# A decoder trunk on one core: early splits of two weights in buffers of their own, and a first chunk loaded in halves

## The chip, the core and the metric

The kernel runs on one core of one Trainium2 chip. The metric is the device time of one execution in microseconds (us), as the median of several executions. TensorE (PE) multiplies matrices, and PEld is its loading of weights; ScalarE (ACT), VectorE (DVE) and GpSimd (POOL) compute on tiles; SyncE (SP) issues most transfers. Each engine works through its instructions in the order in which the program lists them, and waits on semaphores for what other engines or transfers owe it.

## The reference, cut to what matters

Two layers of a decoder with 512 tokens of 1024 features: layer 0 mixes tokens with latent attention, layer 1 with a gated recurrence; each goes on through a SwiGLU block and a gated extra embedding. The change lies at the start of layer 0's attention:

```python
down = x @ w_dqkv                                   # 512x1024 @ 1024x576
c_q  = rms_norm(down[..., :256], q_norm)
c_kv = rms_norm(down[..., 256:512], kv_norm)
k_rope = apply_rope(down[..., 512:], cos, sin)      # 64 columns
q = (c_q @ w_uq).reshape(B, S, H, 128 + 64)         # the 64: rotary queries
kv = (c_kv @ w_ukv).reshape(B, S, H, 128 + 128)     # the second 128: values
...
s = (q_nope . k_nope + q_rope . k_rope) * scale     # causal softmax, then @ v, then @ w_o
```

## The kernel before

Every fp32 product is done as three TensorE products of split operands: `split` (L178) makes a rounded copy `hi` on ACT (L179) and the rest `lo = src - hi` on DVE (L180), and `mm3` (L203 to L205) adds hi·hi, lo·hi and hi·lo. A group of weights is one `unit` (L188): a 128x1024 tile `raw` (3 buffers) is loaded by SP (L191) and split into `whi` and `wlo`. These have 5 buffers each, which the chunks of the down projection and all later units take in turn. So a unit's `lo` frees its `raw` buffer for the load three units on, and a unit's `hi` needs the products of the unit five back to be done.

`mla` starts with the down projection. The contraction over 1024 features is cut into 8 chunks (kc) of 128; for each, SP loads `xT` (128x512, L580) and `w_dqkv` (128x576, L582), ACT and DVE split both, and PE adds 8 groups of three 288-column products (4 token tiles t by 2 column halves n) into 8 banks of PSUM (`dq`: tp, tp, sc, sc, ps, ps, ps, wg). The last three chunks (NL = 3) run token tile by token tile (L594 to L596), so that the sums of t = 0 are ready first. In the same loop each tile is normed: ACT squares and sums both halves (L605), DVE and POOL make the inverse root (`rstd`: L211 and L213), DVE scales each half into `cn` (L610) and copies the rotary key (L612, tile `kr`). Two tiles later, `to_feat` (L307) transposes `cn` on PE, and `csink` splits the result into `cT` (ACT L179 and DVE L180, names `big<-tp`).

After that loop the source has the units of rotary queries (`wr`, from `mla_w_qr`) and of values (`wv`, two from `mla_w_v`), then for each t the rotary queries (`rope_q`: 6 products, rotated at L554 to L560) and the values (12 products), and then, head by head, units of `mla_w_qk` (here qk0, qk1, ...), scores and softmax. The rotary tables (L259 to L285) use a sine on ACT, for which a table is loaded (ACT_TABLE_LOAD, 1.28 us).

The code doesn't say when each engine does its share: a scheduler reorders each engine's instructions when the program is built, from dependences, buffers and its own estimates. The order on each engine is fixed from then on. Buffers of the tag "mb" (`mid`) are a second set; before the change the attention uses the first of them for the rotary tables, and the others only for the softmax (`turn`).

## Time and profile before

| what | us |
|---|---|
| median of 3 executions (lowest, highest) | 1292.88 (1292.80, 1293.83) |
| the profiled execution, own time | 1295.24 |
| its span, first to last instruction | 1293.5 |
| PE busy in it (share of the span) | 1269.2 (98%) |
| DVE, ACT, POOL busy | 802.1 (62%), 665.7 (51%), 128.0 (10%) |
| PE waits before its first product | 5.6 |
| PE waits between 11 and 42 us (norms of the down projection) | 0.48 and 1.29 |

The profiled execution took 2.36 us more than the median; differences are worked out within it and then applied to the median. PE is the engine that sets the time, so the question at each step is when PE stands still and what releases it.

### The profile page before, as it was taken

Reading aid. Unit: us, or ns where it says so; the run is one execution under the profiler, and the core shown is the slowest. Engines: PE = TensorE matmul, PEld = TensorE weight load, DVE = VectorE, ACT = ScalarE, POOL = GpSimd, SP = SyncE. Lnnn points to the kernel's source line nnn. Section 1 sums busy time; section 2 is a strip of 40 time slices with the busy share of each in tenths; the row PEclk is TensorE's granted clock in tenths of the full one; section 3 lists DMA queues with packets and bytes.
Section 4 is the critical chain, followed back from the end, with each engine's and each line's share of the span. In section 5 each row is a group of like instructions: output and inputs, shape, how many; then the busy total and the mean of one; then the engine's idle time right before and its main releaser. Section 6 shows DMA issues by size and latency. Waiting matters only on the chain.

```text
span 1293.5 us, 20112 instructions
## 1 busy us (share of the span) xinstructions
PE 1269.2 (98%) x7900; PEld 1138.4 (88%) x7900; DVE 802.1 (62%) x1454; ACT 665.7 (51%) x1150; POOL 128.0 (10%) x165
## 2 busy tenths in 40 slices
PE   8999999999999999999999999999999999999998
PEld 8778879999999888888888888888899999888887
DVE  7998477777765333853367778358676676433463
ACT  6666367776775222533334344337677766322352
POOL 0200021111110000100001110002111111000000
PEclk9999999999999999999999999999999999999999
DMA  7124157878775223232321222337888886323231
GB/s 229 66 66 138 47 142 172 203 185 184 175 186 153 92 94 111 93 111 69 116 96 51 64 82 66 97 83 157 215 185 187 185 185 160 126 94 96 92 98 49
DMA packets 49055, 161.70 MB, mean 125 GB/s; under 512 B 5824, under 2 KB 6080, under 8 KB 48704
## 3 DMA queue, kind: packets, MB, share of 16 engines
q1 hardware_dynamic: 36000, 123.71, 29.9%
q0 software_dynamic: 12960, 36.71, 16.4%
q8 instruction: 62, 1.02, 0.3%
q14 instruction: 33, 0.27, 0.1%
HBM read 158.30 MB, written 2.10 MB: 124 GB/s over the span
## 4 chain that ended last, share of the span: by engine, by line
PE 86%; DVE 5%; DMA 4%; ACT 2%; issue 2%; POOL 1%; SPq 0%; POOLq 0%; DVEq 0%; ACTq 0%
PE ps L203 19%; PE ps L204 19%; PE ps L205 19%; PE sc L203 3%; PE sc L204 3%; PE sc L205 3%; PE wg L204 3%; PE wg L203 3%; PE wg L205 2%; DMA raw<-ffn_w_in 2%; PE sc L859 2%; PE tp L307 2%; PE ps L433 2%; DMA wlo<-ffn_w_in 2%; PE tp L204 2%
## 5 line engine op out<-in xcount | busy, mean ns | idle before, releaser
L180 DVE TENSOR_TENSOR wlo<-raw,whi 128x1024 fp32r<-128x1024 f32 (+1 forms) x125 | 149.2, 1195 | 206.7 <-ACT whi L179 204.3
L179 ACT ACTIVATE whi<-raw 128x1024 fp32r<-128x1024 f32 (+1 forms) x125 | 129.4, 1036 | 242.2 <-PE wg L205 125.6
L203 PE MATMUL ps<-big,whi 128*128 128x256 f32 (+1 forms) x640 | 202.3, 316 | 1.7 <-ACT part L444 1.7
L205 PE MATMUL ps<-big,wlo 128*128 128x256 f32 (+1 forms) x640 | 198.7, 311 | 0.0
L204 PE MATMUL ps<-big,whi 128*128 128x256 f32 (+1 forms) x640 | 198.7, 310 | 0.0
L203 PE MATMUL ps<-whi,big 128*128 128x512 f32 (+2 forms) x440 | 171.1, 389 | 0.5 <-ACT t L605 0.5
L205 PE MATMUL ps<-whi,big 128*128 128x512 f32 (+2 forms) x440 | 168.2, 382 | 0.0
L204 PE MATMUL ps<-wlo,big 128*128 128x512 f32 (+2 forms) x440 | 167.9, 382 | 0.0
L203 PEld LDWEIGHTS ps<-big,whi 128*128 128x128 f32 x640 | 122.4, 191 | 6.7 <-ACT part L444 1.9
L205 PEld LDWEIGHTS ps<-big,wlo 128*128 128x128 f32 x640 | 122.2, 191 | 6.5
L204 PEld LDWEIGHTS ps<-big,whi 128*128 128x128 f32 x640 | 122.4, 191 | 4.8
L205 PEld LDWEIGHTS ps<-whi,big 128*128 128x128 f32 x440 | 83.0, 189 | 16.0
L203 PEld LDWEIGHTS ps<-whi,big 128*128 128x128 f32 x440 | 83.1, 189 | 14.9 <-ACT t L605 0.7
L204 PEld LDWEIGHTS ps<-wlo,big 128*128 128x128 f32 x440 | 83.1, 189 | 14.4
L180 DVE TENSOR_TENSOR wlo<-ma,whi 128x1024 fp32r<-128x1024 f32 x40 | 49.0, 1224 | 35.4 <-ACT whi L179 35.4
L213 POOL TENSOR_TENSOR rr<-rv,mhalf 128x1 f32<-128x1 f32 (+2 forms) x28 | 27.9, 997 | 419.5 <-DVE rv L211 419.5
L205 PE MATMUL ps<-whi,ma 128*128 128x512 f32 x164 | 64.2, 392 | 0.0
L204 PE MATMUL ps<-wlo,ma 128*128 128x512 f32 x164 | 64.2, 391 | 0.0
L203 PE MATMUL ps<-whi,ma 128*128 128x512 f32 x164 | 64.0, 390 | 0.0
L186 POOL DMA_DIRECT2D ma<-ffn_w_in x40 | 34.3, 857 | 246.6 <-DVE big L465 158.0
L444 ACT ACTIVATE part<-ps 128x256 f32<-128x256 f32 x120 | 44.4, 374 | 25.8 <-PE ps L205 25.2
L184 ACT ACTIVATE whi<-raw 128x1024 fp32r<-128x1024 f32 x50 | 52.8, 1061 | 7.7 <-DMA raw<-ffn_w_in 4.3
(325 smaller groups left out, 3154.2 us busy)
## 6 DMA issues: line engine op xcount, KB each, us to landing
raw<-ffn_w_in SPq DMA_DIRECT2D x88, 512.0 KB, 5.0
wlo<-ffn_w_in POOLq DMA_DIRECT2D x48, 512.0 KB, 7.3
raw<-ffn_w_down SPq DMA_DIRECT2D x44, 512.0 KB, 3.5
ma<-ffn_w_in POOLq DMA_DIRECT2D x40, 256.0 KB, 6.9
raw<-ple_w_gate SPq DMA_DIRECT2D x16, 512.0 KB, 3.6
raw<-hgrn_w_fq SPq DMA_DIRECT2D x16, 512.0 KB, 3.6
raw<-mla_w_o SPq DMA_DIRECT2D x8, 512.0 KB, 3.6
raw<-hgrn_w_v SPq DMA_DIRECT2D x8, 512.0 KB, 4.4
```

Of the source, the lines that this page charges most:

```text
L179: self.nc.scalar.activation(hi, src, AF.Copy)
L180: self.nc.vector.tensor_tensor(out=lo, in0=src, in1=hi.bitcast(F32), op=ALU.subtract)
L184: self.nc.scalar.activation(hi, raw, AF.Copy)
L186: self.nc.gpsimd.dma_start(lo, src, accum_op=ALU.add)
L203: mm(ps, a[0], b[0], start=start, stop=False, skip_group_check=more)
L204: mm(ps, a[0], b[1], start=False, stop=False, skip_group_check=more)
L205: self.last = mm(ps, a[1], b[0], start=False, stop=stop, skip_group_check=more).ins
L213: nc.gpsimd.tensor_tensor(out=r, in0=v, in1=self.mhalf[:, :n], op=ALU.pow)
L307: self.nc.tensor.transpose(out=ps[:, c * P:(c + 1) * P], in_=src[:, c * P:(c + 1) * P], identity=self.ident)
L433: nc.tensor.matmul(ps[q][:, :N], w[q][k][:, kc * P:(kc + 1) * P], xT(f"A{half + 1}{kc // 4 + 1}")[m][:, kc % 4], start=kc + k + m == 0, st ...
L444: copy = lambda dst, src: nc.scalar.activation(dst, src[:, :N], AF.Copy)
L859: nc.tensor.matmul(ps[:, c * P:(c + 1) * P], X[:, c * P:(c + 1) * P], pair_view(cs[0][:, :, 1, :], cs[1][:, :, 0, :]), start=True, stop=True)
```

## The change

Two things are edited. First, chunk kc = 0 is loaded in four transfers rather than two, in the order: tokens 0 to 255 of `xT`, columns 0 to 287 of `w_dqkv`, columns 288 to 575, tokens 256 to 511. Each half is split by itself, and PE's 24 products follow in groups of two token tiles and one column half. Second, `unit` takes a tag: the unit of rotary queries and the first unit of values are split into buffers of the tag "mb" instead of `whi` and `wlo`, and both are written ahead of the norm loop; the second unit of values stays where it was.

```diff
@@ -185,12 +185,15 @@
         self.nc.scalar.activation(lo, hi.bitcast(F32), AF.Copy, scale=-1.0)
         self.nc.gpsimd.dma_start(lo, src, accum_op=ALU.add)
 
-    def unit(self, src, adding=False):
+    def unit(self, src, adding=False, tag=None):
 
         raw = self.wp.tile([P, 1024], F32, tag="raw", bufs=3, name=self.nm("raw"))
         self.nc.sync.dma_start(raw, src)
-        hi = self.wp.tile([P, 1024], F32R, tag="whi", bufs=5, name=self.nm("whi"))
-        lo = self.wp.tile([P, 1024], F32R, tag="wlo", bufs=5, name=self.nm("wlo"))
+        if tag:
+            hi, lo = self.mid([P, 1024], F32R, tag), self.mid([P, 1024], F32R, tag)
+        else:
+            hi = self.wp.tile([P, 1024], F32R, tag="whi", bufs=5, name=self.nm("whi"))
+            lo = self.wp.tile([P, 1024], F32R, tag="wlo", bufs=5, name=self.nm("wlo"))
         if adding:
             self.split_dma(hi, lo, raw, src)
         else:
@@ -577,13 +580,27 @@
         ws = []
         for kc in range(KC):
             xk = xr[kc // 4][:, kc % 4]
+            raw = self.wp.tile([P, 576], F32, tag="raw", bufs=3, name=self.nm("raw"))
+            w = [self.wp.tile([P, 576], F32R, tag=g, bufs=5, name=self.nm(g)) for g in ("whi", "wlo")]
+            ws.append(w)
+            if kc == 0:
+
+                tok, col = (slice(0, 256), slice(256, 512)), (slice(0, 288), slice(288, 576))
+                for z, src, cs in ((xk, i["xT"][:, 0], tok[0]), (raw, i["mla_w_dqkv"][0], col[0]),
+                                   (raw, i["mla_w_dqkv"][0], col[1]), (xk, i["xT"][:, 0], tok[1])):
+                    nc.sync.dma_start(z[:, cs], src[:, cs])
+                    if z is xk:
+                        self.split(*xT(0, cs), xk[:, cs])
+                    else:
+                        self.split(w[0][:, cs], w[1][:, cs], raw[:, cs])
+                for ts, n in (((0, 1), 0), ((0, 1), 1), ((2, 3), 0), ((2, 3), 1)):
+                    for t in ts:
+                        self.mm3(dq[t][n][:, :288], xT(0, slice(t * P, (t + 1) * P)), [z[:, col[n]] for z in w], True, False)
+                continue
             nc.sync.dma_start(xk, i["xT"][:, kc])
-            raw = self.wp.tile([P, 576], F32, tag="raw", bufs=3, name=self.nm("raw"))
             nc.sync.dma_start(raw, i["mla_w_dqkv"][kc])
             self.split(*xT(kc), xk)
-            w = [self.wp.tile([P, 576], F32R, tag=g, bufs=5, name=self.nm(g)) for g in ("whi", "wlo")]
             self.split(w[0], w[1], raw)
-            ws.append(w)
             if kc < KC - NL:
                 for t in range(NT):
                     down(kc, t, w)
@@ -594,6 +611,8 @@
         cT = [self.slot([P, 4, S], F32R) for _ in range(2)]
         csink = lambda t, n, ps: self.split(*(z[:, :, t * P:(t + 1) * P] for z in cT), ps)
         cns = []
+        wr = self.unit(i["mla_w_qr"], tag="mb")
+        wv = [self.unit(i["mla_w_v"][0], tag="mb")]
         for t in range(NT):
             for kc in range(KC - NL, KC):
                 down(kc, t, ws[kc])
@@ -617,8 +636,7 @@
 
         qs = [self.slot([P, 4, S], F32R) for _ in range(2)]
         vt = (Rows(self, F32R), Rows(self, F32R))
-        wr = self.unit(i["mla_w_qr"])
-        wv = [self.unit(i["mla_w_v"][n]) for n in range(2)]
+        wv.append(self.unit(i["mla_w_v"][1]))
 
         def rope_q(t):
             ps = self.bank()
```

The helpers move down by 3 lines: L178 to L213 stay in the split and become L206 to L208 (`mm3`), L214 and L216 (`rstd`), L310 (`to_feat`), L624 (squares), L629 (scaling), L631 (copy), L288 (sine).

What the scheduler makes of it differs from the kernel before only in the first 440 or so of PE's 7,000 rows, and on ACT and DVE in the rows up to the attention; POOL's order is the same, and SP's has one more load at the start. Three places:

ACT, from the last split of the down projection to the first split of `cT`. In the kernel before (`whi_513` are the rotary-query weights, `whi_519` and `whi_525` the two units of values, `tp_105` and `tp_106` the sums of t = 0, `sc` of t = 1, `ps_109` and `ps_110` of t = 2):

```order
L179 ACTIVATE whi_513<-raw_511 128x1024
L179 ACTIVATE whi_519<-raw_517 128x1024
L285 ACT_TABLE_LOAD
L285 ACTIVATE mb_218<-ma_219 128x128
L605 ACTIVATE t_54_386,ss_385<-tp_105 128x256
L605 ACTIVATE t_54_386,ss_385<-tp_106 128x256
L285 ACTIVATE mb_218<-ma_219 128x128
L605 ACTIVATE t_59_417,ss_416<-sc_107 128x256
L605 ACTIVATE t_59_417,ss_416<-sc_108 128x256
L605 ACTIVATE t_65_455,ss_454<-ps_109 128x256
L605 ACTIVATE t_65_455,ss_454<-ps_110 128x256
L179 ACTIVATE big_365<-tp_447 128x4x128
```

and after the change (`mb_375`: rotary queries, `mb_381`: first values, `whi_531`: second values, `whi_750`: qk0):

```order
L624 ACTIVATE t_60_404,ss_403<-tp_105 128x256
L288 ACT_TABLE_LOAD
L288 ACTIVATE mb_224<-ma_225 128x128
L179 ACTIVATE mb_375<-raw_373 128x1024
L624 ACTIVATE t_60_404,ss_403<-tp_106 128x256
L288 ACTIVATE mb_224<-ma_225 128x128
L179 ACTIVATE mb_381<-raw_379 128x1024
L624 ACTIVATE t_65_435,ss_434<-sc_107 128x256
L179 ACTIVATE whi_531<-raw_529 128x1024
L624 ACTIVATE t_65_435,ss_434<-sc_108 128x256
L179 ACTIVATE big_371<-tp_465 128x4x128
L179 ACTIVATE whi_750<-raw_748 128x1024
```

The squares of t = 0 stood behind both early splits and the table load, one after another; now the first of them comes first, the splits stand between the squares, and the split of qk0, a load that comes later, ends this piece and stands right ahead of the squares of t = 2 (`ps_109`, `ps_110`), which are the next two rows.

DVE, around the scaling of t = 2 (`ps_109`, `ps_110`), before:

```order
L211 TENSOR_SCALAR rv_458<-ss_454 128x2
L610 SCALAR_TENSOR_TENSOR t_68_462<-ps_109,rr_460,ma_98 128x256
L180 TENSOR_TENSOR big_366<-tp_447,big_365 128x4x128
L612 COPY ma_364<-ps_109 128x32
L610 SCALAR_TENSOR_TENSOR t_68_462<-ps_110,rr_460,ma_98 128x256
L612 COPY ma_364<-ps_110 128x32
L180 TENSOR_TENSOR wlo_526<-raw_523,whi_525 128x1024
L180 TENSOR_TENSOR wlo_745<-raw_742,whi_744 128x1024
L180 TENSOR_TENSOR big_366<-tp_485,big_365 128x4x128
L211 TENSOR_SCALAR rv_496<-ss_492 128x2
```

and after (`wlo_751` is qk0's `lo`):

```order
L180 TENSOR_TENSOR big_372<-tp_465,big_371 128x4x128
L214 TENSOR_SCALAR rv_476<-ss_472 128x2
L180 TENSOR_TENSOR wlo_751<-raw_748,whi_750 128x1024
L629 SCALAR_TENSOR_TENSOR t_74_480<-ps_109,rr_478,ma_98 128x256
L631 COPY ma_370<-ps_109 128x32
L629 SCALAR_TENSOR_TENSOR t_74_480<-ps_110,rr_478,ma_98 128x256
L631 COPY ma_370<-ps_110 128x32
L180 TENSOR_TENSOR big_372<-tp_503,big_371 128x4x128
```

The second values' and qk0's `lo` came behind the scaling of t = 2; now they come ahead of it: qk0's is between the statistics (`rv_476`) and the scaling, and the second values' was moved further up, ahead of the scaling of t = 1.

PE, around the transposes of t = 2, before (`ps_531` are rotary queries of tile 0, `ps_547` and `ps_556` its values, `tp_565` and `tp_606` the transposes of t = 2 and 3):

```order
L203 MATMUL ps_547<-whi_519,big_365 128x512
L204 MATMUL ps_547<-wlo_520,big_365 128x512
L205 MATMUL ps_547<-whi_519,big_366 128x512
L203 MATMUL ps_547<-whi_519,big_365 128x512
L204 MATMUL ps_547<-wlo_520,big_365 128x512
L205 MATMUL ps_547<-whi_519,big_366 128x512
L307 MATMUL tp_565<-ident,t_68_462 128x128 x4
L307 MATMUL tp_606<-ident,t_74_500 128x128 x2
L203 MATMUL ps_556<-whi_525,big_365 128x512
L204 MATMUL ps_556<-wlo_526,big_365 128x512
```

and after (`tp_503`: t = 1, `tp_571`: t = 2, `ps_537` and `ps_553`: rotary queries and first values of tile 0):

```order
L206 MATMUL wg_112<-whi_362,big_103 128x288
L207 MATMUL wg_112<-wlo_363,big_103 128x288
L208 MATMUL wg_112<-whi_362,big_104 128x288
L310 MATMUL tp_503<-ident,t_68_442 128x128 x4
L310 MATMUL tp_571<-ident,t_74_480 128x128 x2
L206 MATMUL ps_537<-mb_375,big_371 128x512
L207 MATMUL ps_537<-mb_376,big_371 128x512
L208 MATMUL ps_537<-mb_375,big_372 128x512
L206 MATMUL ps_537<-mb_375,big_371 128x512
L207 MATMUL ps_537<-mb_376,big_371 128x512
L208 MATMUL ps_537<-mb_375,big_372 128x512
L206 MATMUL ps_553<-mb_381,big_371 128x512
```

Before, the transposes of t = 2 came behind the twelve products of rotary queries and first values; now their first two stand ahead of these, right behind the four of t = 1. The transposes of t = 0 (`tp_465`) moved the other way, by nine products, and stand in two pairs with two products between them.

## Rows read from the trace of the kernel before

**Rows 1.** The page's chain of work that ended last, followed back from the end: shares of the span by engine.

```profile
PE 86%; DVE 5%; DMA 4%; ACT 2%; issue 2%; POOL 1%; SPq 0%; POOLq 0%; DVEq 0%; ACTq 0%
```

**Rows 2.** The view of waits of PE over the whole span (rows of four; columns: what waited, for whom, us in all, times, longest).

```profile
PE ps L433 <- DMA wlo<-ffn_w_in: 6.0, 4, 2.9
...
PE tp L307 <- DVE ma L612: 1.3, 1, 1.3
```

**Rows 3.** The timeline of the first 11 us (columns: start, duration, engine, line, operation, out<-in, shape, and in brackets the idle time before and what ended it; L179 is the `hi` split, L180 the `lo`).

```profile
0.74 0.39 SPq L580 DMA_DIRECT2D big<-xT  x1
...
1.18 0.42 SPq L582 DMA_DIRECT2D raw<-mla_w_dqkv  x1
...
4.19 0.63 ACT L179 ACTIVATE big<-big 128x512 fp32r<-128x512 f32 x1 [1.96 <-DMA big<-xT]
...
4.88 0.68 ACT L179 ACTIVATE whi<-raw 128x576 fp32r<-128x576 f32 x1
...
5.62 0.85 PE L203 MATMUL tp<-whi,big 128*128 128x288 f32 x2 [5.62 <-ACT whi L179]
...
7.87 0.76 DVE L180 TENSOR_TENSOR wlo<-raw,whi 128x576 fp32r<-128x576 f32 x1 [0.92 <-ACT whi L179]
...
9.69 0.44 PE L204 MATMUL ps<-wlo,big 128*128 128x288 f32 x1
...
9.93 0.34 PE L205 MATMUL ps<-whi,big 128*128 128x288 f32 x1
...
10.78 0.29 PE L205 MATMUL wg<-whi,big 128*128 128x288 f32 x1
...
10.92 0.30 PE L203 MATMUL tp<-whi,big 128*128 128x288 f32 x1
```

**Rows 4.** The timeline from 22 to 34 us, the norms of t = 0 and t = 1 (same columns; `t<-tp` at L605 is a square of t = 0, L610 a scaling, L307 a group of four transposes).

```profile
24.21 1.23 DVE L180 TENSOR_TENSOR wlo<-raw,whi 128x1024 fp32r<-128x1024 f32 x1 [0.38 <-ACT whi L179]
...
24.86 1.06 ACT L179 ACTIVATE whi<-raw 128x1024 fp32r<-128x1024 f32 x1 [0.69 <-DMA raw<-mla_w_v]
...
25.46 2.45 SPq L191 DMA_DIRECT2D raw<-mla_w_qk  x2
25.58 0.29 PE L205 MATMUL tp<-whi,big 128*128 128x288 f32 x1
...
25.95 1.28 ACT L285 ACT_TABLE_LOAD   x1
...
27.24 0.31 ACT L285 ACTIVATE mb<-ma 128x128 f32<-128x128 f32 x1
...
27.46 0.37 ACT L605 ACTIVATE t<-tp 128x256 bf16<-128x256 f32 x1
...
27.95 0.38 ACT L605 ACTIVATE t<-tp 128x256 bf16<-128x256 f32 x1
...
28.58 0.16 DVE L211 TENSOR_SCALAR rv<-ss 128x2 f32<-128x2 f32 x1
...
28.82 0.71 POOL L213 TENSOR_TENSOR rr<-rv,mhalf 128x2 f32<-128x2 f32 x1 [27.02 <-DVE rv L211]
...
29.57 0.48 DVE L610 SCALAR_TENSOR_TENSOR t<-tp,rr,ma 128x256 f32<-128x256 f32 x1 [0.83 <-POOL rr L213]
...
30.92 0.60 PE L307 MATMUL tp<-ident,t 128*128 128x128 f32 x4
...
33.74 0.60 PE L307 MATMUL tp<-ident,t 128*128 128x128 f32 x4
```

**Rows 5.** The timeline from 34 to 40 us, with the two stops of PE after the down projection (same columns; `ps<-whi,big` of 512 columns are products of rotary queries and values, L612 copies the rotary key out of a PSUM bank).

```profile
34.49 0.18 DVE L612 COPY ma<-ps 128x32 f32<-128x32 f32 x1
...
34.82 0.47 PE L203 MATMUL ps<-whi,big 128*128 128x512 f32 x1 [0.48 <-ACT t L605]
...
35.07 2.36 DVE L180 TENSOR_TENSOR wlo<-raw,whi 128x1024 fp32r<-128x1024 f32 x2
...
37.66 0.60 PE L307 MATMUL tp<-ident,t 128*128 128x128 f32 x4
...
38.18 0.70 POOL L213 TENSOR_TENSOR rr<-rv,mhalf 128x2 f32<-128x2 f32 x1 [4.73 <-DVE rv L211]
...
38.91 0.48 DVE L610 SCALAR_TENSOR_TENSOR t<-ps,rr,ma 128x256 f32<-128x256 f32 x1 [0.49 <-POOL rr L213]
...
39.55 0.41 PE L307 MATMUL tp<-ident,t 128*128 128x128 f32 x2 [1.29 <-DVE ma L612]
```

**Rows 6.** The view of transfers in the first 60 us (columns: tile<-tensor, queue, operation, times, size of one, median us from issue to landing).

```profile
raw<-mla_w_qk SPq DMA_DIRECT2D x4, 512.0 KB, 4.2
...
raw<-mla_w_o SPq DMA_DIRECT2D x1, 512.0 KB, 3.6
```

**Rows 7.** Busy time in stretches of the span (columns: stretch, its length, busy us and instructions of PE, PEld, DVE, ACT and POOL, the clock granted to PE as a share of 2.4 GHz, share of time and rate of the transfers).

```profile
70.00:130.00 60.00, 59.28 (x368) 49.26 (x367) 51.47 (x169) 39.49 (x116) 1.04 (x1) 1.00 0.29 95
194.00:198.00 4.00, 4.00 (x24) 4.00 (x23) 1.14 (x2) 1.93 (x3) 0.00 (x0) 0.57 0.08 14
890.00:892.00 2.00, 2.00 (x20) 2.00 (x19) 0.00 (x0) 0.63 (x2) 0.00 (x0) 1.00 0.97 195
```

**Rows 8.** The timeline of PE at two long stops in the SwiGLU blocks (columns as in rows 3).

```profile
193.63 1.50 PE L433 MATMUL ps<-big,wlo 128*128 128x256 f32 x8 [2.88 <-DMA wlo<-ffn_w_in]
...
888.57 1.21 PE L433 MATMUL ps<-big,wlo 128*128 128x256 f32 x8 [2.47 <-DMA wlo<-ffn_w_in]
```

## The prediction

> **What bounds the kernel now.** I read the chain of work that ended last first: 86% of it is TensorE (PE) [rows 1]. PE's order is fixed when the program is built, so a change is worth what it takes from, or adds to, the times at which PE stands still. The view of waits says where those are: 5.6 us ahead of the first product, 6.0 us for weights in the SwiGLU blocks, and in the part that the change touches one of 1.3 us [rows 2]; the timeline adds one of 0.48 us [rows 5]. From the first product to 34 us there is none, which is the cover under which all norms of the first two token tiles run today. 1293.5 us of span contain some 1269 us of PE work, and the change alters none of that.
>
> **The start.** PE's first product needs `xT` and the `hi` of the first weights. The loads are issued at 0.74 and 1.18; `xT`'s `hi` starts at 4.19 and the weights' at 4.88, 0.69 later, takes 0.68, and PE starts at 5.62 [rows 3]. With halves the first product needs only 288 columns. Their `hi` is about half of 0.68, or 0.37 if I take a 256-column ACT row (a square [rows 4]), so 0.31 is saved whatever the transfers do. The transfers: 544 KB lie ahead of the first product before, 272 KB after; half of the 0.69 between the two landings is 0.35 if they share the rate evenly, none if the landing is set by latency alone, and the whole 0.69 at most. So PE starts 0.3 to 1.0 us earlier; I take 0.7 (0.31 + 0.35, rounded). The Trainium skill (DMA: Bandwidth & Descriptors, section "Measured (HBM→SBUF, 128 partitions, SWDGE, issued from GpSimd)") speaks against this edit: it asks to batch transfers to 1 MiB or more, since smaller ones lose rate. If that ruled here, the halves would land no sooner than the wholes, 0.3 would be left of the 0.7, and the sum below would be +2.0. The rows speak for overlap instead: two loads issued 0.44 apart land 0.69 apart, both over 3 us after their issue.
>
> A second doubt is the clock. PE's products start 0.24 us apart at 9.69 and 9.93, and 0.14 apart at 10.78 and 10.92 [rows 3]: the granted clock goes from 1.2 to 2.4 GHz at about 10 us. If that moment moves with PE's start, all of the 0.7 is kept; if it stands still, the extra work is done at 1.2 GHz and half is kept. Bounds of the term: **-0.2 to -1.0, taken -0.7**. Two more SP issues at some 0.45 us push all later loads of the projection back by 0.9. The cover: chunk 1 is split by 7.87 + 0.76 = 8.63 and first used at 10.92 [rows 3], 2.3 us of slack, of which 1.6 (0.9 and the earlier start) is used up, so nothing is lost. Without cover it would cost those 0.9.
>
> **The two stops of today go: -1.77.** The 0.48 us stop is before the first 512-column product at 34.82, whose PSUM bank is freed by the key copy of t = 2 at 34.49 + 0.18 [rows 5]. The 1.29 us stop is before the transposes of t = 3 at 39.55; behind it stands a chain of 2.36 us of `lo` splits on DVE from 35.07, ahead of the statistics, POOL's 0.70 and the scaling at 38.91 [rows 5]. In the new order neither place exists as it was. What is late next is worked out now, from the same rows, with PE 0.7 earlier.
>
> **The new chain of the norms.** t = 0's last product is 25.58 + 0.29 - 0.7 = 25.2 [rows 4]. ACT then does: square (0.49 from 27.46 to 27.95) to 25.7, table load 1.28 to 27.0, sine (0.22 to its next) 27.2, `hi` of rotary queries 1.06 to 28.25, second square 28.75, second sine 29.0, `hi` of first values 30.0. Before the change both `hi` were over when the squares began; now 1.06 of split stands between the two squares of t = 0, whose sum feeds one statistic. DVE: `lo` of rotary queries 1.23 to 29.5; statistic 29.7; POOL 0.71 to 30.5; first scaling to 31.0; then `lo` of first values, 1.23, to 32.2, which the new order puts between the two scalings; second scaling to 32.7.
>
> PE comes to the transposes of t = 0 at 30.92 - 0.7 + 9 products of 0.135 = 31.4: the first pair is ready. The second pair, two products and 0.3 of transposes later, is due at 32.0 and ready at 32.7: **0.7 new wait**. For t = 1, seven products on, PE is due at 32.7 + 0.3 + 0.9 = 33.9. DVE's statistic is at 32.9, but the `lo` of the second values (1.23) stands ahead of the scalings: 34.2, first pair 34.7, second 35.2: 0.8 and 0.2 of wait, of which I take **0.8** in all, since one DVE instruction begins up to 0.1 before the other ends.
>
> t = 2 is the dear one. Its transposes now come right behind those of t = 1, where PE is at 35.3; before, twelve products stood between (34.82 to 37.66, 2.84 us [rows 5]). Its squares wait on ACT behind qk0's `hi`. qk0's load needs the `raw` buffer that the `lo` of rotary queries frees: in the trace the load is issued at 25.46, as that `lo` ends (24.21 + 1.23) [rows 4]. Now that `lo` ends at 29.5, so the load lands 3.6 to 4.2 us later [rows 6], at 33.1 to 33.7. ACT is then free of `cT`'s first split at about 33.6; `hi` to 34.7, two squares to 35.7. DVE has `cT`'s `lo` in between, statistic at 36.1, then qk0's `lo`, 1.23, to 37.3 (POOL's 0.70 runs beside it), scaling to 37.8. PE has been idle since 35.3: 2.5 by this sum, **taken 2.3** with the same overlaps. On ACT's queue behind the waiting `hi` are those squares, qk1's `hi` and `cT`; nothing else of PE's hangs on them in that time.
>
> t = 3: PE goes on with the twelve products, is due at 37.6 + 0.3 + 2.84 + 0.3 = 41.0; on ACT, qk1's and qk2's `hi`, one each ahead of a square, and on DVE qk1's `lo` make the scaling ready at 41.3 to 42.0: 0.3 to 1.0, **taken 0.6**. Together **+4.4** (3.4 to 5.2), against 1.77 before.
>
> **Later.** `whi` and `wlo` are free of two units, so the splits of `mla_w_qk` run ahead. From 70 to 130 us PE stands still for 60.00 - 59.28 = 0.72 [rows 7]. Some of it is such splits: -0.3 taken, -0.7 at best; +0.5 (the size of a stop like that of [rows 5]) if the new order makes one more.
>
> **The sum:** -0.7 - 1.77 + 4.4 - 0.3 = +1.63. The profiled execution of 1295.24 becomes 1296.9; the median of 1292.88 becomes **1294.5**.
>
> **Rivals.** (a) The chain keeps up: the squares and scalings are early enough and only the gains stay: -0.7 - 1.77 = -2.5, 1290.4. For it: today's chain shows slack, as t = 0's scaling at 29.57 is 1.3 ahead of PE at 30.92 [rows 4]. Against: three instructions of over 1 us that stood before or behind this chain now stand in it. (b) Old stops turn into new ones of the same size, and only the start is gained: 1292.2; this needs t = 2's stop to be 0.3 or less in place of 2.3, so the load of qk0 early or its `hi` short. (c) The slower end: t = 2's stop lowers PE's clock. After a stop of 2.88 us the granted clock was 0.57 over 4 us [rows 7, 8], so 4 x 0.43 = 1.7 us were lost; after one of 2.47 us it stayed at 1.00 [rows 7, 8]. At 2.3 it stays; this rival decides from somewhere between these two, and with the waits of 0.7 and 0.8 shortly before it could do so sooner: +1.63 + 1.7 = +3.3, 1296.2. (d) The loads of qk0 and qk1 land later than the 3.9 that I took in the middle of 3.6 and 4.2 (these are medians of four loads and of one, 0.6 apart [rows 6]): at 0.5 more for each, both stops behind them grow, +1.0, 1295.5.
>
> **How the numbers follow.** Forecast 0.50, (a) 0.12, (b) 0.12, (c) 0.13, (d) 0.13. A measurement of this kernel can tell 0.2%, 2.6 us, from no change: below 1290.3 is faster, above 1295.5 slower. Faster: half of (a), 0.06. Slower: (c), half of (d), and 0.03 of the forecast's upper end: 0.23. Same: 0.71. The forecast by itself has bounds from -0.3 (smallest waits, best start) to +3.0, with 1293.3 to 1295.8 as its likely part; the range of 8 in 10 leaves out (a) and the far end of (c) and (d): 1291.9 to 1296.6.
>
> **What would show it.** PE's first product at 4.6 to 5.3 and the clock's step. Then PE waits on L310 (transposes), released by DVE, four of them or more between 30 and 42 us with 4.4 in sum, the longest of 2 to 2.5 us just ahead of the rotary queries; qk0's load issued near 29.5; its `hi` waiting for it, and t = 2's squares behind. No wait of that size there, or the squares ahead of 34 us, would make the forecast wrong; a granted clock near 0.5 after 38 us would show (c), a longer wait of ACT for `raw` (d).

## The result, and the profile after

| what | before | after |
|---|---|---|
| median of 9 executions (lowest, highest), us | 1292.70 (1291.57, 1293.83) | 1295.62 (1293.48, 1297.20) |
| ratio of the times, 95% interval | | 1.0029 (1.0020 to 1.0037) |
| the profiled execution, own time (its span) | 1295.24 (1293.5) | 1294.68 (1292.9) |
| PE's first product / first product at 2.4 GHz | 5.62 / 10.11 | 3.90 / 8.61 |
| PE waits between 11 and 42 us | 0.48, 1.29 | 0.75, 0.85, 2.62 |
| granted clock from 34 to 46 us | 1.00 | 0.72 |
| first SwiGLU product | 182.31 | 185.17 |

The changed kernel is 0.29% slower, 2.9 us. Its one profiled execution is shorter than the profiled one of before, though, and this has to be cleared up first. PE's waits for `ffn_w_in` in the SwiGLU blocks, which the change doesn't touch, were 6.0 us before [rows 2] and are 3.8 now, and these waits vary from execution to execution (2.9 to 6.0 in the twelve profiles of this document). So I compare the two traces only up to the first product of the first SwiGLU block, where the changed kernel is 185.17 - 182.31 = 2.86 us behind.

The view of PE's waits over the whole span, after, and the timeline of PE at the first product of the SwiGLU block, before (L433) and after (L436):

```profile
PE ps L436 <- DMA wlo<-ffn_w_in: 3.8, 3, 2.2
```

```profile
182.31 2.16 PE L433 MATMUL ps<-big,whi 128*128 128x256 f32 x16
185.17 2.16 PE L436 MATMUL ps<-big,whi 128*128 128x256 f32 x16
```

The timeline of PE at the start, before (L203) and after, and the view of the loads of the first 1.6 us, two before and two after (last column: us from issue to landing):

```profile
10.11 0.30 PE L203 MATMUL ps<-whi,big 128*128 128x288 f32 x1
...
3.90 0.61 PE L206 MATMUL tp<-whi,big 128*128 128x288 f32 x1 [3.90 <-ACT whi L179]
...
8.16 0.44 PE L208 MATMUL ps<-whi,big 128*128 128x288 f32 x1
8.40 0.37 PE L206 MATMUL ps<-whi,big 128*128 128x288 f32 x1
8.61 0.29 PE L207 MATMUL ps<-wlo,big 128*128 128x288 f32 x1
8.74 0.29 PE L208 MATMUL ps<-whi,big 128*128 128x288 f32 x1
```

```profile
raw<-mla_w_dqkv SPq DMA_DIRECT2D x1, 288.0 KB, 3.7
big<-xT SPq DMA_DIRECT2D x1, 256.0 KB, 3.4
...
raw<-mla_w_dqkv SPq DMA_DIRECT2D x1, 144.0 KB, 2.2
big<-xT SPq DMA_DIRECT2D x1, 128.0 KB, 2.2
```

The first load of weights is issued at 1.18 in both kernels and lands 2.2 us later as a half, 3.7 as a whole: 1.48 earlier from the unrounded times. The `hi` split behind it is 0.24 shorter (from its start to the first product 0.50, before 0.74 [rows 3]). Together they make the first product 1.72 us earlier, at 3.90 in place of 5.62 [rows 3]. Products start 0.24 apart up to 8.40 and 0.13 apart from 8.61; before, they are 0.24 apart up to 9.93 [rows 3], and the next is at 10.11. So the clock rises 1.5 us earlier.

The timeline from 23 to 43 us, all engines, after (behind 37.60 PE alone):

```profile
23.92 0.29 PE L208 MATMUL tp<-whi,big 128*128 128x288 f32 x1
...
24.25 0.38 ACT L624 ACTIVATE t<-tp 128x256 bf16<-128x256 f32 x1 [2.75 <-PE tp L208]
...
29.12 0.29 PE L208 MATMUL ps<-whi,big 128*128 128x288 f32 x1
...
31.36 0.41 PE L310 MATMUL tp<-ident,t 128*128 128x128 f32 x2 [0.75 <-DVE ma L631]
...
31.69 1.22 DVE L180 TENSOR_TENSOR wlo<-raw,whi 128x1024 fp32r<-128x1024 f32 x1
...
31.86 1.61 POOL L216 TENSOR_TENSOR rr<-rv,mhalf 128x2 f32<-128x2 f32 x1 [2.40 <-DVE rv L214]
...
32.30 0.60 ACT L179 ACTIVATE big<-tp 128x512 fp32r<-128x512 f32 x1 [1.82 <-PE tp L310]
...
32.79 1.05 ACT L179 ACTIVATE whi<-raw 128x1024 fp32r<-128x1024 f32 x1
...
33.74 0.38 ACT L624 ACTIVATE t<-ps 128x256 bf16<-128x256 f32 x1
...
34.05 0.93 PE L310 MATMUL tp<-ident,t 128*128 128x128 f32 x4 [0.85 <-DVE t L629]
...
34.24 0.38 ACT L624 ACTIVATE t<-ps 128x256 bf16<-128x256 f32 x1
...
34.49 0.68 DVE L180 TENSOR_TENSOR big<-tp,big 128x512 fp32r<-128x512 f32 x1
...
35.09 0.16 DVE L214 TENSOR_SCALAR rv<-ss 128x2 f32<-128x2 f32 x1
35.16 1.22 DVE L180 TENSOR_TENSOR wlo<-raw,whi 128x1024 fp32r<-128x1024 f32 x1
35.33 1.60 POOL L216 TENSOR_TENSOR rr<-rv,mhalf 128x2 f32<-128x2 f32 x1 [1.86 <-DVE rv L214]
...
36.97 0.48 DVE L629 SCALAR_TENSOR_TENSOR t<-ps,rr,ma 128x256 f32<-128x256 f32 x1 [0.59 <-POOL rr L216]
...
37.60 0.66 PE L310 MATMUL tp<-ident,t 128*128 128x128 f32 x2 [2.62 <-DVE ma L631]
37.91 0.78 PE L206 MATMUL ps<-mb,big 128*128 128x512 f32 x1
...
42.96 0.49 PE L310 MATMUL tp<-ident,t 128*128 128x128 f32 x3
```

The last product of t = 0's first column half starts at 23.92, before the change at 25.58 [rows 4]: the start gave 1.66. ACT squares the first half of t = 0 at 24.25, and then loads the sine's table (24.75) and splits the rotary queries (26.26) before the second half, so POOL's root is only at 28.75, hardly earlier than before (28.82 [rows 4]). Three stops of PE follow. The first (0.75) is put down to the key copy of t = 0 (at 31.03 on DVE), behind the `lo` of first values. The second (0.85) ends with the scaling of t = 1: the `lo` of the second values stands right behind its statistic (31.69), and POOL's root, beside it from 31.86, takes 1.61 in place of 0.71. The third (2.62) is t = 2's. PE had the first sums of t = 2 ready at 29.41 (29.12 + 0.29), but ACT squares them only at 33.74 and 34.24: ahead in its queue stands `cT`'s first split, which waits for PE's transposes until 32.30, and then qk0's `hi` of 1.05. Even so, ACT is done with them at 34.71, and DVE comes to their statistic only at 35.09, behind the scaling of t = 1 and `cT`'s `lo` (34.49). So the squares are late but had 0.4 to spare, and the stop is made on DVE and POOL: from the statistic on, DVE has qk0's `lo` (35.16) and POOL its root beside it (1.60), and the scaling begins at 36.97, 1.88 after the statistic. There is no stop for t = 3.

Busy time in stretches of 2 us, after (columns as in rows 7; the one ahead of the transfers' share is the granted clock):

```profile
36.00:38.00 2.00, 0.40 (x3) 0.43 (x3) 1.41 (x6) 1.38 (x4) 0.93 (x1) 0.50 0.52 98
38.00:40.00 2.00, 2.00 (x7) 1.61 (x6) 1.89 (x4) 0.72 (x3) 1.00 (x1) 0.50 0.55 209
40.00:42.00 2.00, 2.00 (x6) 1.52 (x6) 1.41 (x7) 1.06 (x1) 0.60 (x1) 0.50 0.33 76
42.00:44.00 2.00, 2.00 (x11) 1.60 (x10) 1.24 (x5) 0.84 (x2) 1.43 (x2) 0.83 0.46 186
```

From 36 to 42 us PE works at half of 2.4 GHz, and in the next stretch it comes back. In the kernel before the granted clock is 1.00 over the whole of 34 to 46.

**The ledger up to the SwiGLU block**, in the two profiled executions: start -1.66; old stops gone -1.77; new stops +4.22, and another +0.33 inside the group at 34.05 (0.93 for four transposes that take 0.60 [rows 4]). Later, the attention is quicker: with the same 760 products and transposes left, PE is at 43.71 before and at 47.32 after, and needs 138.60 us and 137.85 us from there to the SwiGLU block, -0.75. That makes +0.37, and 2.86 - 0.37 = +2.49 is left. PE's work after the third stop (37.60 on) runs at 1.2 GHz until about 42.7 (0.83 of a stretch of 2 us is 1.32 at full and 0.68 at half), 5.1 us in which at most half, 2.5, is lost. The loss can be seen directly: the twelve products behind the stop take 37.91 to 42.96, 5.05 us, and twelve of the same shape took 2.84 before (34.82 to 37.66 [rows 5]), 2.21 less. So the 2.49 are the clock's, as near as a remainder can show.

### The profile page after: what moved, and what is told of

The parts are those of the page before. It is cut to its first block, busy times and chain, and to the rows that moved or that the text cites. A ratio compares the mean times of both kernels' runs of the same rounds, so it can differ in the third digit from the quotient of the medians.

```text
span 1292.9 us, 20106 instructions
## 1 busy us (share of the span) xinstructions
PE 1271.3 (98%) x7900; PEld 1140.2 (88%) x7900; DVE 802.3 (62%) x1456; ACT 666.4 (52%) x1152; POOL 129.3 (10%) x165
## 4 chain that ended last, share of the span: by engine, by line
PE 86%; DVE 4%; DMA 4%; ACT 3%; issue 1%; POOL 1%; DVEq 0%; POOLq 0%; ACTq 0%; SPq 0%
PE ps L206 19%; PE ps L207 19%; PE ps L208 19%; PE sc L206 3%; PE sc L207 3%; PE sc L208 3%; DMA raw<-ffn_w_in 3%; PE wg L207 3%; PE wg L206 2%; PE wg L208 2%; PE tp L206 2%; PE sc L877 2%; PE tp L207 2%; PE tp L208 2%; PE tp L310 2%
## 5 line engine op out<-in xcount | busy, mean ns | idle before, releaser
L180 DVE TENSOR_TENSOR wlo<-raw,whi 128x1024 fp32r<-128x1024 f32 (+2 forms) x124 | 146.8, 1185 | 205.6 <-ACT whi L179 203.3
L179 ACT ACTIVATE whi<-raw 128x1024 fp32r<-128x1024 f32 (+2 forms) x124 | 127.5, 1029 | 239.4 <-PE wg L208 125.5
L206 PE MATMUL ps<-big,whi 128*128 128x256 f32 (+1 forms) x640 | 202.5, 316 | 0.7 <-ACT part L447 0.7
L208 PE MATMUL ps<-big,wlo 128*128 128x256 f32 (+1 forms) x640 | 198.7, 311 | 0.0
L206 PE MATMUL ps<-whi,big 128*128 128x512 f32 (+2 forms) x424 | 164.5, 388 | 0.0
L208 PE MATMUL ps<-whi,big 128*128 128x512 f32 (+2 forms) x424 | 162.0, 382 | 0.0
L207 PE MATMUL ps<-wlo,big 128*128 128x512 f32 (+2 forms) x424 | 161.7, 381 | 0.0
L208 PEld LDWEIGHTS ps<-big,wlo 128*128 128x128 f32 x640 | 122.2, 191 | 6.4
L206 PEld LDWEIGHTS ps<-big,whi 128*128 128x128 f32 x640 | 122.4, 191 | 5.9 <-ACT part L447 0.9
L208 PEld LDWEIGHTS ps<-whi,big 128*128 128x128 f32 x424 | 79.9, 189 | 15.2
L207 PEld LDWEIGHTS ps<-wlo,big 128*128 128x128 f32 x424 | 80.2, 189 | 13.9
L206 PEld LDWEIGHTS ps<-whi,big 128*128 128x128 f32 x424 | 80.2, 189 | 13.8
L180 DVE TENSOR_TENSOR wlo<-ma,whi 128x1024 fp32r<-128x1024 f32 x40 | 49.0, 1224 | 35.7 <-ACT whi L179 35.7
L216 POOL TENSOR_TENSOR rr<-rv,mhalf 128x1 f32<-128x1 f32 (+2 forms) x28 | 29.0, 1035 | 420.0 <-DVE rv L214 420.0
L208 PE MATMUL ps<-whi,ma 128*128 128x512 f32 x164 | 64.2, 392 | 0.0
L206 PE MATMUL ps<-whi,ma 128*128 128x512 f32 x164 | 64.0, 390 | 0.0
L186 POOL DMA_DIRECT2D wlo<-ffn_w_in x48 | 41.4, 863 | 153.7 <-ACT wlo L185 80.3
```

The costliest lines, as they stand in the source:

```text
L179: self.nc.scalar.activation(hi, src, AF.Copy)
L180: self.nc.vector.tensor_tensor(out=lo, in0=src, in1=hi.bitcast(F32), op=ALU.subtract)
L186: self.nc.gpsimd.dma_start(lo, src, accum_op=ALU.add)
L206: mm(ps, a[0], b[0], start=start, stop=False, skip_group_check=more)
L207: mm(ps, a[0], b[1], start=False, stop=False, skip_group_check=more)
L208: self.last = mm(ps, a[1], b[0], start=False, stop=stop, skip_group_check=more).ins
```

## The experiments

Each kernel ran in several rounds beside the kernel before on its chip. One table holds the numbers of all; "mean clock" is that of the whole span, as the mean over all executions of a kernel, and the next column counts the executions in which it was 0.997 or less. These two columns count low stretches anywhere in the span (the profile of before has one behind 194 us [rows 7]); where they lie is known for the one profiled execution of each kernel.

| kernel | ratio (95% interval) | first product | stops, 11 to 42 us | clock 34 to 46 | first SwiGLU product | mean clock | at 0.997 or less |
|---|---|---|---|---|---|---|---|
| before | | 5.62 | 0.48, 1.29 | 1.00 | 182.31 | .9989 | 7 of 93 |
| after | 1.0029 (1.0020 to 1.0037) | 3.90 | 0.75, 0.85, 2.62 | 0.72 | 185.17 | .9962 | 8 of 9 |
| e1_halves | 0.9995 (0.9984 to 1.0005) | 3.91 | 0.92, 1.29 | 1.00 | 181.74 | .9992 | 1 of 12 |
| e2_early | 1.0012 (1.0004 to 1.0021) | 5.46 | 0.36, 3.00 | 0.86 | 184.58 | .9978 | 3 of 11 |
| e3_mb_late | 1.0000 (0.9991 to 1.0010) | 3.92 | 0.25, 2.62 | 0.72 | 184.16 | .9974 | 6 of 12 |
| e4_filler | 1.0008 (0.9999 to 1.0017) | 3.90 | 0.76, 0.85, 0.88 | 1.00 | 184.16 | .9993 | 0 of 11 |
| e5_qk0_behind | 1.0023 (1.0012 to 1.0034) | 4.06 | 0.75, 0.86, 1.89 | 0.86 | 185.71 | .9978 | 6 of 12 |
| e6_both_behind | 1.0023 (1.0008 to 1.0038) | 3.99 | 0.75, 0.86, 1.28 | 0.86 | 184.49 | .9975 | 7 of 12 |
| e7_lo_cut | 1.0005 (0.9995 to 1.0016) | 3.91 | 0.75, 0.32, 2.32 | 0.86 | 184.51 | .9982 | 3 of 12 |
| e8_halves_bounds_later | 0.9994 (0.9982 to 1.0006) | 3.99 | 0.96, 0.47 | 1.00 | 180.65 | .9992 | 1 of 12 |
| e9_halves_cut | 0.9992 (0.9983 to 1.0001) | 3.97 | 0.37, 0.30, 0.66 | 1.00 | 180.60 | .9989 | 1 of 11 |
| e10_changed_again | 1.0026 (1.0012 to 1.0040) | 4.19 | 0.76, 0.85, 2.62 | 0.72 | 186.18 | .9966 | 10 of 12 |

**The theory**: the early units hurt, by the stops of t = 0, 1 and 2 and by the clock that falls behind them, and the halves gain about 1 us. The rivals: the halves themselves cost something later; or the lost 2.5 us are not the clock's; or it is the buffers of "mb" and not the early place that matters.

**e1_halves: the halves alone** (units in their old place and buffers).

```diff
-        wr = self.unit(i["mla_w_qr"], tag="mb")
-        wv = [self.unit(i["mla_w_v"][0], tag="mb")]
         for t in range(NT):
...
-        wv.append(self.unit(i["mla_w_v"][1]))
+        wr = self.unit(i["mla_w_qr"])
+        wv = [self.unit(i["mla_w_v"][n]) for n in range(2)]
```

> Only the halves of the first chunk; both weights are split as in the kernel before (whi and wlo, after the norm loop). Theory (the start gains 1.7, the stops in the norms and a granted clock of 0.50 after the longest of them cost more): PE starts at 3.9, the two old stops stay and grow by what the start gained (about 0.9 and 1.5 in place of 0.48 and 1.29), the clock stays at 1.00 after them: 0.3 to 0.9 us faster than the kernel before. Rival (the loss comes with the start, by transfers in another rhythm): 2 us or more slower than before, as the whole change.

The clock stays at 1.00 and the SwiGLU block is reached 0.57 earlier than before: the sums of t = 0 are done 1.01 earlier in this profile, not 1.66, and the timeline of PE shows a first stop of 0.92, where before it was 0.48 [rows 5], and the old 1.29:

```profile
34.25 0.47 PE L206 MATMUL ps<-whi,big 128*128 128x512 f32 x1 [0.92 <-DVE ma L629]
...
38.98 0.41 PE L310 MATMUL tp<-ident,t 128*128 128x128 f32 x2 [1.29 <-DVE ma L629]
```

The projection is done sooner, but t = 1's and t = 2's norms, behind splits on ACT and DVE, are not. So part of the start's gain, 0.44, comes back as a longer stop. I had expected 0.3 to 0.9 us less time; the ratio's interval holds that and no change as well.

**e2_early: the early units alone** (chunk 0 in whole loads again).

```diff
-            if kc == 0:
...
-                continue
             nc.sync.dma_start(xk, i["xT"][:, kc])
+            raw = self.wp.tile([P, 576], F32, tag="raw", bufs=3, name=self.nm("raw"))
             nc.sync.dma_start(raw, i["mla_w_dqkv"][kc])
```

> Only the early splits in buffers of their own; the first chunk is loaded whole. Theory: PE starts at 5.6; stops of 0.6 for the transposes of t = 0 or 1 and about 3 us for those of t = 2, then a granted clock of 0.50 for some 6 us: 4 to 5 us slower than before. Rival without a price of the clock: the stops alone, 2.3 us slower. Rival in which the early splits are harmless: within 1 us of before.

Slower, as expected in sign, with a longest stop of 3.00, but by some 1.6 us and not the 4 to 5 that I had set down: in the profile the clock is low only half as long (0.86 in place of 0.72). The stops of t = 0 and t = 1 shrink to one of 0.36, because PE comes later.

**e3_mb_late: halves, and the units in "mb" buffers, but written behind the norm loop.**

```diff
-        wr = self.unit(i["mla_w_qr"], tag="mb")
-        wv = [self.unit(i["mla_w_v"][0], tag="mb")]
         for t in range(NT):
...
         vt = (Rows(self, F32R), Rows(self, F32R))
+        wr = self.unit(i["mla_w_qr"], tag="mb")
+        wv = [self.unit(i["mla_w_v"][0], tag="mb")]
         wv.append(self.unit(i["mla_w_v"][1]))
```

> Halves, and both weights in buffers of their own, but written after the norm loop. Theory: the order of ACT and DVE is still set by when buffers come free, so qk0's split stands ahead of t = 2's scaling again; a stop of 2.5 to 2.8 us for the transposes of t = 2 and the clock at 0.50 behind it: 2 to 3 us slower than before. Rival (the place in the source is what costs): like the halves alone, 0.3 to 0.9 faster than before.

The timeline of ACT, DVE and PE around the longest stop:

```profile
31.55 0.38 ACT L622 ACTIVATE t<-ps 128x256 bf16<-128x256 f32 x1
...
33.67 0.16 DVE L214 TENSOR_SCALAR rv<-ss 128x2 f32<-128x2 f32 x1
33.74 1.22 DVE L180 TENSOR_TENSOR wlo<-raw,whi 128x1024 fp32r<-128x1024 f32 x1
...
35.55 0.48 DVE L627 SCALAR_TENSOR_TENSOR t<-ps,rr,ma 128x256 f32<-128x256 f32 x1 [0.59 <-POOL rr L216]
...
36.18 0.66 PE L310 MATMUL tp<-ident,t 128*128 128x128 f32 x2 [2.62 <-DVE ma L629]
```

The stop of 2.62 stays without the early place: the buffers are enough for it. The lost time doesn't stay: I had expected 2 to 3 us more than before, and the ratio is 1.0000. The early place adds the stops of t = 0 and t = 1 (0.75 and 0.85 after the change, one of 0.25 here). And the squares aren't in the chain, which corrects my theory: here t = 2's squares start at 31.55, 2.2 us earlier than after the change, with no split of qk0 ahead of them, and the stop is the same. What is late is DVE, which has the `lo` of first values at 30.27 in t = 1's chain and the second values' at 33.74 in t = 2's. From such a `lo` to the scaling behind it 1.81 us go by (33.74 to 35.55, and 35.16 to 36.97 after the change); without one, the scaling came 0.99 after the statistic (28.58 to 29.57 [rows 4]). Its executions fall into two equal groups: six with a mean clock of 0.997 or less, median 1294.2, and six above, median 1291.7 (though one of these is at 1294.9). The profiled one was the longest of all twelve. The gap of 2.5 us is the size that the ledger gave the clock, but the mean clock doesn't say in which stretch it was low, and e5, which has two groups of six as well, shows a gap of 1.0 (1295.6 and 1294.6).

**e4_filler: the changed kernel with t = 1's four transposes done five times**, 16 products that write the same values again, ahead of the long stop.

```diff
-        for c in range(4):
+        for c in list(range(4)) * times:
...
-                self.to_feat(cns[t - 2], csink, t - 2, 0)
+                self.to_feat(cns[t - 2], csink, t - 2, 0, 5 if t == 3 else 1)
```

> The changed kernel, and the four transposes of t = 1 issued five times over (16 more, the same values), which the order puts right into the long stop ahead of t = 2's transposes; all else in the same order. Theory (the clock falls in that stop): PE's idle time there is under 1 us, the granted clock stays at 1.00, and the kernel is 2 to 2.7 us faster than the changed one, so 0.3 to 1 us slower than before. Rival (the clock costs nothing here, PE only waits for the chain anyway): the same as the changed kernel, 2.9 us slower than before.

The timeline of PE and the busy time in stretches (columns as above):

```profile
34.70 2.68 PE L310 MATMUL tp<-ident,t 128*128 128x128 f32 x20 [0.85 <-DVE t L629]
38.25 0.41 PE L310 MATMUL tp<-ident,t 128*128 128x128 f32 x2 [0.88 <-DVE ma L631]
```

```profile
36.00:38.00 2.00, 1.38 (x13) 1.14 (x11) 1.41 (x2) 1.27 (x5) 1.59 (x1) 1.00 0.43 170
38.00:40.00 2.00, 1.75 (x9) 1.53 (x10) 2.00 (x7) 1.32 (x4) 0.56 (x1) 1.00 0.94 252
40.00:42.00 2.00, 1.91 (x11) 1.41 (x10) 1.41 (x5) 1.32 (x2) 1.05 (x1) 1.00 0.30 57
```

PE's 20 transposes take 2.68, 1.75 more than the four of the changed kernel; the third stop is 0.88 in place of 2.62, and the clock stays at 1.00. PE starts behind the stop 0.65 us later than after the change (38.25, 37.60), and still it is 1.0 us earlier at the SwiGLU block; counted from the first square of t = 0 (24.90 here, 24.25 there), it is 159.26 against 160.92, 1.66 less with 16 products more. The ratio falls from 1.0029 to 1.0008. So the stretch at 1.2 GHz costs some 1.7 us or more, and of all that the changed kernel does, PE's standing still is enough to explain it: the order on DVE and POOL is the same here, and on ACT but for one pair behind the squares of t = 2.

**e5_qk0_behind: qk0's `hi` held behind t = 2's squares** (it takes a bias, a zero worked out from their sums).

```diff
+            self.nc.scalar.activation(hi, src, AF.Identity, bias=nil)
...
+            if t == 2:
+                nil = self.small([P, 1], tag="nil", bufs=1)
+                nc.vector.tensor_scalar(out=nil, in0=ss[:, 1:2], scalar1=0.0, scalar2=None, op0=ALU.mult)
```

> The changed kernel, with qk0's hi split made to need the squares of t = 2 (a bias of zero worked out from them), so that it stands behind them on ACT. Theory (the long stop is the sum of what the order put ahead of t = 2's scaling, qk0's hi being 0.95 of it, and a stop of 2.6 us is what lowers the clock): the stop ahead of t = 2's transposes is 1.8 to 2.1 in place of 2.6, the granted clock stays at 1.00, about 2 us faster than the changed kernel. If the clock falls all the same: 0.3 to 0.8 faster than it. Rival (t = 2's chain is set by DVE and POOL, ACT's order is covered): the stop stays at 2.6.

The timeline of DVE and POOL:

```profile
35.93 0.15 DVE L217 TENSOR_SCALAR rv<-ss 128x2 f32<-128x2 f32 x1
36.17 0.70 POOL L219 TENSOR_TENSOR rr<-rv,mhalf 128x2 f32<-128x2 f32 x1 [1.92 <-DVE rv L217]
...
37.03 0.47 DVE L635 SCALAR_TENSOR_TENSOR t<-ps,rr,ma 128x256 f32<-128x256 f32 x1
```

The third stop is 1.89, 0.73 less, but not because the squares are earlier: DVE takes their statistic 1.10 after PE's transposes of t = 1 began (34.83 to 35.93), and after the change it was 1.04 (34.05 to 35.09). What is shorter is the way from the statistic to the scaling, 1.10 in place of 1.88: with qk0's `hi` its `lo` has moved back too, and the root takes 0.70 in place of 1.60. So ACT's order is covered, as the rival of this expectation had it, though the stop didn't stay at its 2.6. The clock falls, against the expectation, and the ratio doesn't show the gain.

**e6_both_behind: `cT`'s first split held back too.** The edit of e5, and t = 0's transposes split with the same bias, behind t = 2's squares.

```diff
+            if t == 2:
...
+                self.to_feat(cns[0], lambda t, n, ps: csink(t, n, ps, nil), 0, 0)
```

> The changed kernel, with qk0's hi split and the hi split of t = 0's transposes both made to need the squares of t = 2, so these squares have nothing in front of them that waits. Theory (the queue on ACT holds squares that are ready): the squares of t = 2 come at about 31 in place of 33.7, the stop for t = 2 is 1.2 to 1.6, the clock stays at 1.00, about 2 us faster than the changed kernel. Rival (t = 2's chain is set by DVE and POOL): the stop stays above 2.

The timeline of ACT, DVE, POOL and PE:

```profile
30.77 0.38 ACT L625 ACTIVATE t<-ps 128x256 bf16<-128x256 f32 x1
...
34.96 0.16 DVE L217 TENSOR_SCALAR rv<-ss 128x2 f32<-128x2 f32 x1
35.20 0.70 POOL L219 TENSOR_TENSOR rr<-rv,mhalf 128x2 f32<-128x2 f32 x1 [1.32 <-DVE rv L217]
...
36.66 0.77 PE L209 MATMUL ps<-mb,big 128*128 128x512 f32 x1 [1.28 <-DVE ma L638]
```

Now t = 2's squares start at 30.77, 3 us earlier than after the change, and yet PE's last stop is still 1.28: DVE takes their statistic only at 34.96, in its queue behind the work on t = 1. The 1.34 that the stop lost can't be put down to ACT's queue: here `cT`'s `lo` no longer stands ahead of the statistic on DVE nor qk0's behind it, the root takes 0.70, and PE's order differs, with the twelve products ahead of t = 2's transposes and the stop ahead of the first of them. The stop is as short as expected, but the clock falls even so, and the 2 us that I had expected to gain don't show.

**e7_lo_cut: the `lo` of the second values, qk0 and qk1 in two halves of 512 columns.**

```diff
+            self.nc.scalar.activation(hi, raw, AF.Copy)
+            for c in (slice(0, 512), slice(512, 1024)):
+                self.nc.vector.tensor_tensor(out=lo[:, c], in0=raw[:, c], in1=hi[:, c].bitcast(F32), op=ALU.subtract)
```

> The changed kernel, with the lo of the second values, qk0 and qk1 done by two DVE instructions of 512 columns in place of one of 1024, which may stand apart. Theory (POOL's small root can't go on while a long DVE split runs, and ends some 0.55 after it): roots beside a 512-column split take up to 1.1 to 1.2 us in place of 1.6, roots beside none 0.7; the stops get shorter for t = 1, and t = 2's stays about 2.5, since ACT's order stands. Rival (POOL is only slowed in proportion to DVE's work): the roots still take 1.6 wherever a split is beside them.

The timeline of DVE and POOL:

```profile
32.15 0.68 DVE L202 TENSOR_TENSOR wlo<-raw,whi 128x512 fp32r<-128x512 f32 x1
32.32 1.08 POOL L220 TENSOR_TENSOR rr<-rv,mhalf 128x2 f32<-128x2 f32 x1 [2.39 <-DVE rv L218]
...
35.69 0.68 DVE L180 TENSOR_TENSOR big<-tp,big 128x512 fp32r<-128x512 f32 x1
35.85 0.70 POOL L220 TENSOR_TENSOR rr<-rv,mhalf 128x2 f32<-128x2 f32 x1 [2.46 <-DVE rv L218]
```

A root beside a half of 0.68 takes 1.08. The one of t = 2 takes 0.70, with a `lo` of the same size and time beside it, but `cT`'s, one of whose inputs lies in PSUM. The stops of t = 1 and t = 2 fall by 0.53 and 0.30, the clock is low for half as long in the profile, and the ratio comes down to 1.0005. Its interval lies below the changed kernel's first one (from 1.0020), though it meets that of e10 (from 1.0012).

**e8_halves_bounds_later: e1 with `lower_bounds`, a small computation for layer 1, moved to layer 1.**

```diff
-        self.lower_bounds(lg)
+        self.lg = lg
...
     def hgrn(self, xT):
+        self.lower_bounds(self.lg)
```

> The halves of the first chunk alone, with the code of the recurrence's lower bounds moved into the second layer, which gives another order on ACT in the norms: both hi splits of rotary queries and first values first, then t = 0's squares, then the table load. Theory (with the clock at 1.00, time is start plus stops): stops in the norms of 0.4 us in all in place of 1.8, and the earlier start: 1.5 to 3 us faster than the kernel before, and faster than the halves alone by 1 us. Rival (stops saved there come back later in the attention): like the halves alone.

The second stop falls from 1.29 to 0.47, but the first stays (0.96): 1.4 in all, where I had expected 0.4. The SwiGLU block is reached 1.1 us earlier than in e1; the time can't be told from e1's, nor from that of the kernel before.

**e9_halves_cut: e1 with the `lo` of values, qk0 and qk1 cut as in e7, and the transposes of t - 2 written behind the squares and scaling of t.**

```diff
-            if t >= 2:
-                self.to_feat(cns[t - 2], csink, t - 2, 0)
             ss = self.small([P, 2], tag="ss")
...
             cns.append(cn)
+            if t >= 2:
+                self.to_feat(cns[t - 2], csink, t - 2, 0)
```

> A version to beat both: the halves of the first chunk; rotary queries and values split in whi and wlo as before; the lo of these three units, qk0 and qk1 in two DVE instructions of 512 columns; the transposes written one step later in the norm loop. Theory (time is start, stops and clock): PE starts at 3.9, stops in the norms of about 1.5 us in all, one stop fewer in the attention, the clock at 1.00: 1.5 to 3.5 us faster than the kernel before. Rival (what a shorter stop saves comes back as another): like the halves alone, 0.3 to 0.9 faster.

(The rotary queries, which the expectation counts among the three, are not cut.) No stop is longer than 0.66, and the SwiGLU block is reached 1.7 us earlier than before. It has the lowest ratio here, 0.9992, but the interval (0.9983 to 1.0001) just holds no change, and it can't be told from e1 and e8. The 1.5 to 3.5 us that I had expected are not shown.

**e10_changed_again: the changed kernel once more, on the chip and beside the runs of e9.**

> The changed kernel as it is, again, beside the version above. Theory: the stops of 0.75, 0.85 and 2.6 us come back to within 0.1, the granted clock falls in the third again, and the time is 2.5 to 3.5 us over the kernel before; PE's first product at 3.9 again, with the clock rising anywhere from 8 to 10.3. Rival (the fall of the clock in the profiled execution was an accident): the clock stays at 1.00, and the time is 1 to 1.5 over before.

1.0026, so slower in a second set of runs as well, by the 2.5 to 3.5 us that were expected, with the same stops and the clock low in the profile again; in 10 of 12 executions the mean clock is 0.997 or less. Those have a median of 1295.5, the other two of 1292.3.

## Why the prediction was right, and where its sizes were off

**The sign and the mechanism held.** The forecast was +1.6 us by three new stops that outweigh two old ones and the earlier start; +2.9 was measured, inside the range and near the top of the forecast's likely part. The size is partly luck: without the clock, which the forecast left at nothing, the measured terms make +0.8, and what lifts them to 2.9 is rival (c)'s mechanism. The chances leaned to the wrong side, though: "within 0.2%" had 0.71, and the 0.29% (0.20 to 0.37) that were measured had 0.23. e1, without the units, is not slower; e2, without the halves, is: the units cost, and the halves alone don't.

**The three stops** were predicted as 0.7, 0.8 and 2.3 and measured as 0.75, 0.85 and 2.62, at the transposes of the tiles named; the first came ahead of the first pair of t = 0, not the second. Two errors in t = 2's chain nearly cancel. I had taken ACT's squares, behind qk0's `hi`, for what sets the statistic, at 36.1; qk0's `hi` started 0.8 earlier than by my sum (32.79), the squares had time to spare, and the statistic came at 35.09, when DVE was free. And POOL's root didn't run beside qk0's `lo` at its 0.70 but took 1.60. So DVE and POOL alone make this stop: it is 2.62 in e3 too, with the squares 2.2 us earlier. For t = 3 I had taken 0.6, and there was none: PE came to it late, at half clock. At full clock, in e4, it waits 0.10 there.

**The step that failed is the one that set aside rival (c)**: "At 2.3 it stays", from two single stops, of 2.88 (the clock fell) and 2.47 (it stayed) [rows 7, 8]. I had named the doubt, the stops of 0.7 and 0.8 shortly before, and then gave the case 0.13. With those ahead the clock fell behind stops of 2.62, of 1.89 (e5) and of 1.28 (e6), but not behind 1.29 with only 0.48 ahead (before) or 0.92 ahead (e1). So the size of the longest stop doesn't decide. Nor does their sum by itself: in the SwiGLU blocks the clock fell behind single stops of 2.16 (after, at 192.4 us) and 2.08 (e3, at 195.0), while it stayed behind stops that make 2.49 together (e4) and behind a single one of 2.64 (e9, at 884.1). The price that (c) named, 1.7, was too small by the ledger, 2.49, because the clock stayed low for about 6.8 us, from 35.9 to 42.7, in place of some 3.4 (0.57 over 4 us [rows 7]); e4, which has losses of its own behind the stop, gives 1.66.

**The start** was taken at -0.7, with bounds to -1.0; the profiled execution gave -1.66. The split's share was near (0.31 taken, 0.24 measured). The landing's was not: I had halved the gap between two landings (0.69), and the half landed 1.48 sooner, beyond the 0.69 that I had as the most. The rule of the Trainium skill that I set against this edit (DMA: Bandwidth & Descriptors, section "Measured (HBM→SBUF, 128 partitions, SWDGE, issued from GpSimd)"), to batch transfers, was for another queue. The trace agrees with it on the rate: by issue to landing, 144 KB in 2.2 us is less per us than 288 KB in 3.7. But a lower rate alone doesn't make a half land as late as a whole, as I took it there, and what PE waits for is the first landing. Not all of the earlier first product is kept, as I feared: in the ten profiles with halves it is at 3.90 to 4.19, but the clock's rise at 8.1 to 10.2. The last product of t = 0 (its second column half) starts at 24.32 to 25.10, in the mean at 24.78, against 25.98 and 25.96 with the whole chunk (before and e2): 1.2 is the mean gain.

**"Later" (-0.3) was right in sign and came to -0.75**, the best that I had named (-0.7). The waits that the view lists behind 70 us are the same 0.5 and 0.2 in both traces, so it is gained in steps too small for that view: the 138.60 us of before are 138.60 in e1, which has no units in "mb" buffers, 137.86 in e10 and 137.83 in e3. But e5 and e6, with the same buffers, have 138.99 and 138.65, so the buffers alone don't give it, and no run shows which steps they are.

**The sum, with measured terms**: -1.2 - 1.77 + 4.55 - 0.75 + 2.49 = +3.3, beside 2.9 between the medians. Without the clock it would be +0.83; e4, which keeps the clock, measures +1.0 (0.0008 of 1292).

**What stays open.** What decides whether the clock falls behind a stop, and for how long (half as long in the profiles of e2, e5, e6 and e7). That it falls in the norms in nearly all executions of the changed kernel is likely from the mean clocks (0.997 or less in 18 of 21), but shown only for the two that were profiled. It is open, too, why shorter stops in e5 and e6 leave no mark on the median. Nor did a run tell apart why the buffers alone bring the long stop (e3): because the units need not wait for the products that free `whi` and `wlo`, or because those two then have room for the next split.

## What to carry to other kernels

An own buffer for a weight is no gain by itself (the changed kernel gains 0.75 us later in the attention, against 2.8 of new stops less old ones and 2.5 of clock): its split, and those queued behind it, may move into the middle of a short chain (square, statistic, root, scaling) on which the bounding engine is about to wait, so look at what each in-order engine has in front of the short instruction that PE needs, and ask which of these engines is free last (here DVE with POOL, not ACT). When stops of 1 to 3 us stand close together, price the half-clock stretch behind them (1.7 to 2.5 us here) as a likely term, not as a rival. Halving the very first loads shortens the way to the first product, here by 1.72 us, but only a part of this lasts if the norms behind it are paced by other engines, and the time of the halves alone (e1) couldn't be told from that of before.
